# Storing only the combined weight operands of a seven-product FFN: quarters of the weights are loaded raw and split in either half of the sequence

## Chip, cores and metric

One core of a Trainium2 chip runs the whole kernel in one launch. The metric is the device time of a launch in microseconds; lower is better. Engines are named as in the profile: PE is TensorE, DVE VectorE, ACT ScalarE, POOL GpSimd, SP the queue engine that issues the DMAs (SyncE).

## What is computed

One layer of a streaming trunk on x of shape (1, 2048, 1024) in float32, D_FF = 2816:

```
h = rmsnorm(x); u = h @ w_in                       # 1024 -> 1536
y_lru  = rg_lru(conv(u[:512])) * gelu(u[512:1024])
y_pool = pool_mixer(u[1024:])
h_res = x + concat(rmsnorm(y_lru), rmsnorm(y_pool)) @ w_out
h = rmsnorm(h_res)
ff = silu(h @ ffn_w1) * (h @ ffn_w3)               # 1024 -> 2816, twice
out = rmsnorm(h_res + ff @ ffn_w2)                 # 2816 -> 1024
```

The change is in the FFN alone: the three products with `ffn_w1`, `ffn_w3` and `ffn_w2`.

## The kernel before, in words

**Precision.** A float32 product is made of three matmuls on a reduced type (fp32r). Each operand is split into a high part (a copy that rounds, on ScalarE) and a low part (source minus high part, on VectorE); `split` (L231) does that, and `mm3` (L236) multiplies high by high, high by low and low by high into one PSUM bank (L237, L238, L239 in this order).

**FFN.** The 2048 tokens are worked off in two halves (`hf` 0 and 1) of two chunks of 512 tokens. D_FF is cut into 11 column groups `j` of 256 columns (the loop at L893). For each group and half, `ffn_gate` (w1), `ffn_up` (w3) and `ffn2` (w2) each multiply a 2 x 2 block matrix of weights with a 2 x 2 block matrix of activations. They do so with seven block products (numbered n = 0 to 6) where the plain way takes eight, the scheme of Strassen in Winograd's form. The weight operands are the quarters b11, b21 and b22 themselves and four combinations of quarters, t1 to t4, which GpSimd makes by subtracting quarters (`comb`). In `ffn1` (L584, which serves gate and up) the products 0, 2 and 6 take b11, b21 and b22; in `ffn2` (L681) the products 2, 3 and 6 take b11, b21 and b22. VectorE and GpSimd combine the results: u2 and u3 (L630, L632, L636) in `ffn1`, and sums into `acc` and `G` (L706, L710) in `ffn2`; ScalarE brings products out of PSUM (`copy_a`, L224). The last group's w2 (`ffn2_last`, L767) takes four plain products, with four raw quarters.

**Where weights come from.** In half 0 the quarters are loaded raw (`load_raw`, L206, 256 KB each), combined, and split by `split_kept` (L198) into one of four 512 KB slots (pool "wsp", tile w_hl). The split operand is then stored to DRAM (c13_d for w1 and w3, c2_d for w2; c_d in the profile, L203). In half 1 nothing is combined or split: `kept` (L182) reads every operand back from there. Of each seven calls, three read it as two 256 KB halves into the slots for raw quarters (six slots, pool "raw"), the other four into one slot of "wsp" (the tiles w_kept).

**Order.** In the loop over groups the seven products of `ffn2(j)` and of `ffn_gate(j + 1)` alternate ("fg" seven times), after the seven of `ffn_up(j)`. At the change of halves the first products of the next half's gate stand ahead of `ffn2_last`. The order on each engine is made at build time by a list scheduler which simulates the program's time; `tc.high_priority(AHEAD)` raises the priority of splits and evictions by 400 (FIRST: by 1500). So an edit may move instructions on every engine. DMAs are issued by SP in order.

Of the kernel before, what the change touches and what calls it, by code (L numbers as in the profile page):

```python
# [13 lines left out]
ALU = mybir.AluOpType  # L14
# [3 lines left out]
P = 128  # L18
# [3 lines left out]
W = 512  # L22
NB = W // P
# [47 lines left out]
def trunk(ctx: ExitStack, tc: tile.TileContext, xT, w_io, w13, w2, gates, pool_w, w_inT, vecs,  # L71
# [126 lines left out]
    def split_kept(src, cache, prepare=AHEAD, eng=None):  # L198

        w_ = wsp("w_hl", (P, 2, W))  # L200
        with tc.high_priority(prepare):
            split(w_[:, 0], w_[:, 1], src, eng)
        nc.sync.dma_start(cache, w_.bitcast(F32))  # L203
        return w_[:, 0], w_[:, 1]

    def load_raw(src, shape):  # L206
# [377 lines left out]
    def ffn1(hf, j, w, ops, s, after):  # L584
# [3 lines left out]

        def quarter(r, c):
            return load_raw(w13[j, w, r, c], (P, NB, P)).rearrange("p k m -> p (k m)") if hf == 0 else None  # L590

# [7 lines left out]
        def product(n, ps, a, b, fresh):  # L599
            wh, wl = split_kept(b, c13_d[j, w, n]) if hf == 0 else kept(c13_d[j, w, n])  # L600
            for kk in range(NB):
# [4 lines left out]
        X, Y = bank("ps"), bank("ps")  # L606
        b11 = quarter(0, 0)
        product(0, X, A11, b11, True)
# [9 lines left out]
        yield  # L618
        b21 = quarter(1, 0)
        product(2, X, A12, b21, False)  # L620
# [17 lines left out]
        yield  # L638
        product(6, V, S4, b22, False)
        after((V, u2), 1)  # L640
# [40 lines left out]
    def ffn2(hf, j, s, acc, G):  # L681
# [3 lines left out]
        def quarter(r, c):  # L685
            return load_raw(w2[j, r, c], (P, W)) if hf == 0 else None

# [9 lines left out]
        def product(n, banks, a, b, fresh):  # L697
            wh, wl = split_kept(b, c2_d[j, n]) if hf == 0 else kept(c2_d[j, n])
            for dp, ps in enumerate(banks):
# [25 lines left out]
        Y = banks("pY")  # L725
        b22, b12 = quarter(1, 1), quarter(0, 1)
        product(0, Y, operand(half(ALU.subtract, a11, a21)), comb("t3", b22, b12, "r1"), True)
# [29 lines left out]
        yield  # L757
        product(6, V, operand(half(ALU.subtract, a12, s2, s2)), b22, False)
        add(V, c12, "V")
# [7 lines left out]
    def ffn2_last(hf, s, acc):  # L767
# [3 lines left out]
        for h in range(2):  # L771
            for b in range(2):
                cache = c2_d[NP - 1, 2 * h + b]
                ws.append(split_kept(load_raw(w2[NP - 1, b, h], (P, W)), cache, 0) if hf == 0
                          else kept(cache))
        f = {q: operand(s[q], tag) for q, tag in ((2, "f"), (3, "f"), (0, "up" if end else "e"),
# [185 lines left out]
```

## Time and profile before

| | |
|---|---|
| median of 3 runs | 1935.81 us (1935.36 to 1936.9) |
| profiled execution | 1939.97 us, its span 1938.2 us |
| mean granted TensorE clock | 0.977 of full speed |
| PE busy | 1832.8 us, 95% of the span |
| DVE busy | 1355.5 us, 70% |
| POOL busy | 928.5 us, 48% |
| ACT busy | 769.5 us, 40% |
| HBM | 275.36 MB read, 167.77 MB written |

The mixers come first. The FFN's first half runs to about 1200 us, and its second half ends about 50 us before the span does. All durations below come from the profiled execution, which has its own time; the median belongs to other executions of the same kernel. A busy share is an average over stages with different limits, so the rows further down are taken stage by stage: from one steady column group to the next, and around the change of halves.

### The profile page before, as it was taken

How to read it: one execution, taken by the hardware profiler on the slowest of the kernel's cores; microseconds unless marked ns; L12 is line 12 of the kernel's file. 1: busy time of each engine (PE TensorE's matmuls, PEld its weight loads, DVE VectorE, ACT ScalarE, POOL GpSimd, SP SyncE). 2: the span in 40 equal slices, each digit the busy share in tenths (PEclk: the TensorE clock that was granted, in tenths of full speed). 3: DMA queues.
4: the chain of work that ended last, by engine and by line, in shares of the span. 5: the costliest groups of instructions: out<-in, count | busy, mean ns of one | idle time of the engine just before them, and what ended most of it. 6: DMA issues, size and time to landing. Idle time of an engine off the chain costs nothing.

```text
span 1938.2 us, 23419 instructions
## 1 busy us (share of the span) xinstructions
PE 1832.8 (95%) x8016; PEld 1487.6 (77%) x8016; DVE 1355.5 (70%) x2004; ACT 769.5 (40%) x1294; POOL 928.5 (48%) x633
## 2 busy tenths in 40 slices
PE   7989999999988999999999999799999999999996
PEld 5778888787767777777777787577888888888885
DVE  7598499876669778777887878875444445444457
ACT  5463546362334444443444434442322223322223
POOL 3361723332136567666676668373333334432373
PEclk9999999999989999999999999899999999999998
DMA  9956855476987666566656666868555555555552
GB/s 322 321 206 219 323 201 179 148 288 227 394 328 260 227 246 223 217 238 220 245 210 231 230 246 230 313 206 298 186 197 194 195 187 183 201 190 195 195 174 87
DMA packets 160838, 444.69 MB, mean 229 GB/s; under 512 B 17872, under 2 KB 20048, under 8 KB 155728
## 3 DMA queue, kind: packets, MB, share of 16 engines
q1 hardware_dynamic: 160720, 443.20, 64.1%
q8 instruction: 63, 1.03, 0.2%
q14 instruction: 55, 0.45, 0.1%
HBM read 275.36 MB, written 167.77 MB: 229 GB/s over the span
## 4 chain that ended last, share of the span: by engine, by line
PE 69%; DVE 17%; issue 5%; DMA 3%; ACT 2%; POOL 2%; SPq 0%; DVEq 0%; ACTq 0%; POOLq 0%
PE ps L239 17%; PE ps L237 16%; PE ps L238 16%; DVE w_hl L234 3%; PE pV L238 2%; PE pV L239 2%; PE pV L237 2%; PE pX L237 2%; PE pX L238 2%; PE pX L239 2%; DMA c_d<-w_hl 1%; PE pY L237 1%; PE pY L238 1%; PE pY L239 1%; DVE sf L719 1%
## 5 line engine op out<-in xcount | busy, mean ns | idle before, releaser
L710 POOL TENSOR_TENSOR G<-G,e 128x512 f32<-128x512 f32 x152 | 227.8, 1516 | 132.1 <-ACT e L224 129.7
L239 PE MATMUL ps<-h_hi,w_hl 128*128 128x512 f32 x616 | 249.0, 405 | 26.2 <-DVE w_hl L234 26.0
L237 PE MATMUL ps<-h_hi,w_hl 128*128 128x512 f32 x616 | 245.5, 401 | 17.7 <-DVE u L636 10.2
L238 PE MATMUL ps<-h_lo,w_hl 128*128 128x512 f32 x616 | 244.9, 398 | 0.0
L237 PE MATMUL ps<-h_hi,w_kept 128*128 128x512 f32 x616 | 240.9, 392 | 2.0 <-DMA w_kept<-c_d 1.2
L238 PE MATMUL ps<-h_lo,w_kept 128*128 128x512 f32 x616 | 240.9, 391 | 0.0
L239 PE MATMUL ps<-h_hi,w_kept 128*128 128x512 f32 x616 | 238.8, 391 | 0.0
L291 POOL TENSOR_TENSOR sq<-sq 128x512 f32<-128x512 f32 (+1 forms) x71 | 99.7, 1407 | 167.0 <-ACT sq L288 165.6
L239 PEld LDWEIGHTS ps<-h_hi,w_hl 128*128 128x128 f32 x616 | 117.9, 191 | 65.7 <-DVE w_hl L234 40.9
L234 DVE TENSOR_TENSOR f_lo<-sf,f_hi 128x512 fp32r<-128x512 f32 x80 | 92.3, 1154 | 106.8 <-PE pZ L238 37.9
L237 PEld LDWEIGHTS ps<-h_hi,w_hl 128*128 128x128 f32 x616 | 118.0, 191 | 49.6 <-ACT w_hl L224 11.2
L710 POOL TENSOR_TENSOR acc<-acc,e 128x512 f32<-128x512 f32 x80 | 123.3, 1570 | 61.5 <-ACT e L224 60.2
L632 POOL TENSOR_TENSOR u<-u,u 128x512 f32<-128x512 f32 x44 | 66.1, 1502 | 179.2 <-DVE u L630 179.1
L706 DVE TENSOR_TENSOR acc<-pV,acc 128x512 f32<-128x512 f32 x160 | 107.9, 685 | 47.4 <-PE pV L239 46.6
L234 DVE TENSOR_TENSOR w_hl<-raw,w_hl 128x512 fp32r<-128x512 f32 x120 | 130.7, 1091 | 12.1 <-ACT w_hl L224 11.6
L238 PEld LDWEIGHTS ps<-h_lo,w_hl 128*128 128x128 f32 x616 | 118.1, 192 | 25.2
L237 PEld LDWEIGHTS ps<-h_hi,w_kept 128*128 128x128 f32 x616 | 115.8, 188 | 27.8 <-DVE acc L837 1.6
L239 PEld LDWEIGHTS ps<-h_hi,w_kept 128*128 128x128 f32 x616 | 115.7, 188 | 25.4 <-DMA w_kept<-c_d 0.3
L238 PEld LDWEIGHTS ps<-h_lo,w_kept 128*128 128x128 f32 x616 | 115.8, 188 | 25.0
L224 ACT ACTIVATE f_hi<-sf 128x512 fp32r<-128x512 f32 x80 | 50.6, 633 | 202.3 <-DVE sf L719 151.9
L224 ACT ACTIVATE w_hl<-t 128x512 fp32r<-128x512 f32 x96 | 60.3, 628 | 165.6 <-DMA c_d<-w_hl 83.2
L237 PE MATMUL ps<-x_hi,w_kept 128*128 128x512 f32 x288 | 115.0, 401 | 1.4 <-DVE u_g L388 1.4
(359 smaller groups left out, 4520.1 us busy)
## 6 DMA issues: line engine op xcount, KB each, us to landing
c_d<-w_hl SPq DMA_DIRECT2D x228, 512.0 KB, 2.9
w_kept<-c_d SPq DMA_DIRECT2D x130, 512.0 KB, 3.7
w_kept<-c_d SPq DMA_DIRECT2D x196, 256.0 KB, 3.4
w_kept<-cio_d SPq DMA_DIRECT2D x68, 512.0 KB, 3.9
raw<-w SPq DMA_DIRECT2D x132, 256.0 KB, 3.3
w_kept<-cio_d SPq DMA_DIRECT2D x104, 256.0 KB, 3.3
cio_d<-w_hl SPq DMA_DIRECT2D x40, 512.0 KB, 5.2
h_lo<-h_d SPq DMA_DIRECT2D x14, 1024.0 KB, 9.6
```

Source lines behind the costliest of these rows:

```text
L224: return nc.scalar.activation(out, in_, AF.Copy)
L234: (eng or nc.vector).tensor_tensor(lo, src, hi.bitcast(F32), ALU.subtract)
L237: i = nc.tensor.matmul(ps, wh, xh, start=first, stop=False, **kw)
L238: nc.tensor.matmul(ps, wh, xl, start=False, stop=False, **kw)
L239: nc.tensor.matmul(ps, wl, xh, start=False, stop=last, **kw)
L291: eng.tensor_tensor(total, total, sq, ALU.add)
L632: nc.gpsimd.tensor_tensor(u3, u3, u2, ALU.add)
L706: nc.vector.tensor_tensor(dst[dp], ps, dst[dp], ALU.add)
L710: nc.gpsimd.tensor_tensor(dst[dp], dst[dp], e, ALU.add)
L719: nc.vector.tensor_tensor(out, a, b, op)
```

## The change

A new function `operand_w` stands between the products and the two ways of getting a split operand. With a cache it does what was done before: split and store in half 0, read back in half 1. With `None` for a cache it splits the raw quarter into a "wsp" slot and stores nothing, in either half. `None` is given for the products 0, 2 and 6 of `ffn1`, for 2, 3 and 6 of `ffn2`, and for all four operands of `ffn2_last`. In half 1 those quarters are therefore loaded raw again (256 KB where 512 KB were read back) and split again.

```diff
--- before.py
+++ after.py
@@ -202,6 +202,15 @@
             split(w_[:, 0], w_[:, 1], src, eng)
         nc.sync.dma_start(cache, w_.bitcast(F32))
         return w_[:, 0], w_[:, 1]
+
+    def operand_w(hf, b, cache, prepare=AHEAD):
+
+        if cache is None:
+            w_ = wsp("w_hl", (P, 2, W))
+            with tc.high_priority(prepare):
+                split(w_[:, 0], w_[:, 1], b)
+            return w_[:, 0], w_[:, 1]
+        return kept(cache) if hf else split_kept(b, cache, prepare)
 
     def load_raw(src, shape):
         raw = pool.tile(list(shape), F32, name="raw", tag="raw", bufs=N_RAW)
@@ -586,8 +595,11 @@
 
         A11, S3, A12, A22 = ops[0]
 
-        def quarter(r, c):
-            return load_raw(w13[j, w, r, c], (P, NB, P)).rearrange("p k m -> p (k m)") if hf == 0 else None
+        def quarter(r, c, again=False):
+
+            if hf and not again:
+                return None
+            return load_raw(w13[j, w, r, c], (P, NB, P)).rearrange("p k m -> p (k m)")
 
         def comb(name, a, b, tag="up"):
             if hf:
@@ -597,14 +609,14 @@
             return t
 
         def product(n, ps, a, b, fresh):
-            wh, wl = split_kept(b, c13_d[j, w, n]) if hf == 0 else kept(c13_d[j, w, n])
+            wh, wl = operand_w(hf, b, None if n in (0, 2, 6) else c13_d[j, w, n])
             for kk in range(NB):
                 col = slice(kk * P, kk * P + P)
                 mm3(ps, wh[:, col], wl[:, col], a[0][:, kk], a[1][:, kk],
                     fresh and kk == 0, kk == NB - 1, skip_group_check=True)
 
         X, Y = bank("ps"), bank("ps")
-        b11 = quarter(0, 0)
+        b11 = quarter(0, 0, True)
         product(0, X, A11, b11, True)
         u2 = t2("u2", "tm")
         with tc.high_priority(AHEAD):
@@ -616,7 +628,7 @@
         with tc.high_priority(AHEAD):
             copy_a(u3, Y)
         yield
-        b21 = quarter(1, 0)
+        b21 = quarter(1, 0, True)
         product(2, X, A12, b21, False)
         after(X, 0)
         yield
@@ -636,7 +648,7 @@
             nc.vector.tensor_tensor(u3, V, u3, ALU.add)
         after((u3, None), 3)
         yield
-        product(6, V, S4, b22, False)
+        product(6, V, S4, quarter(1, 1, True) if hf else b22, False)
         after((V, u2), 1)
         yield
 
@@ -683,7 +695,7 @@
 
 
         def quarter(r, c):
-            return load_raw(w2[j, r, c], (P, W)) if hf == 0 else None
+            return load_raw(w2[j, r, c], (P, W))
 
         a11, a12, a21, a22 = (s[q] for q in range(4))
 
@@ -695,7 +707,7 @@
             return t
 
         def product(n, banks, a, b, fresh):
-            wh, wl = split_kept(b, c2_d[j, n]) if hf == 0 else kept(c2_d[j, n])
+            wh, wl = operand_w(hf, b, None if n in (2, 3, 6) else c2_d[j, n])
             for dp, ps in enumerate(banks):
                 col = slice(P * dp, P * (dp + 1))
                 mm3(ps, wh[:, col], wl[:, col], a[0], a[1], fresh, True, skip_group_check=True)
@@ -723,7 +735,10 @@
         c11, c12, c21, c22 = acc[0][0:NB], acc[0][NB:], acc[1][0:NB], acc[1][NB:]
 
         Y = banks("pY")
-        b22, b12 = quarter(1, 1), quarter(0, 1)
+        if hf == 0:
+            b22, b12 = quarter(1, 1), quarter(0, 1)
+        else:
+            b22 = b12 = None
         product(0, Y, operand(half(ALU.subtract, a11, a21)), comb("t3", b22, b12, "r1"), True)
         add(Y, c22, "P")
         yield
@@ -755,7 +770,7 @@
         product(5, V, operand(s1), t1, True)
         add(V, c22, "V")
         yield
-        product(6, V, operand(half(ALU.subtract, a12, s2, s2)), b22, False)
+        product(6, V, operand(half(ALU.subtract, a12, s2, s2)), quarter(1, 1) if hf else b22, False)
         add(V, c12, "V")
         yield
 
@@ -770,9 +785,7 @@
         ws = []
         for h in range(2):
             for b in range(2):
-                cache = c2_d[NP - 1, 2 * h + b]
-                ws.append(split_kept(load_raw(w2[NP - 1, b, h], (P, W)), cache, 0) if hf == 0
-                          else kept(cache))
+                ws.append(operand_w(hf, load_raw(w2[NP - 1, b, h], (P, W)), None, 0))
         f = {q: operand(s[q], tag) for q, tag in ((2, "f"), (3, "f"), (0, "up" if end else "e"),
                                                   (1, "up" if end else "f"))}
         scales = []
```

The scheduler's order changes with it. In the rows below a name's number tells tiles apart, and line numbers of the changed kernel are 9 to 12 higher (L234 is L243, L224 is L233, L596 is L608, L632 is L644).

**GpSimd in the first half**, a steady column group, where it makes the combinations of the gate's quarters (t1, t2_) and, with u3, the running sum of `ffn_up`. Before:

```order
L596 TENSOR_TENSOR t1_7084<-raw_6982,raw_6926 128x512
L632 TENSOR_TENSOR u3_6778<-u3_6778,u2_6754 128x512
L596 TENSOR_TENSOR t2__7086<-raw_6980,t1_7084 128x512
L694 TENSOR_TENSOR t4_6958<-raw_6952,t2__6950 128x512
L671 TENSOR_TENSOR s_6688<-s_6688,u3_6778 128x512
```

With the change:

```order
L608 TENSOR_TENSOR t1_7047<-raw_6948,raw_6893 128x512
L608 TENSOR_TENSOR t2__7049<-raw_6946,t1_7047 128x512
L644 TENSOR_TENSOR u3_6747<-u3_6747,u2_6723 128x512
L706 TENSOR_TENSOR t4_6924<-raw_6918,t2__6916 128x512
L683 TENSOR_TENSOR s_6660<-s_6660,u3_6747 128x512
```

The combination t2_ has moved ahead of u3.

**VectorE in the same group**, from the last addition to u3 to the split of the gate's t3 (sf and f are activations on their way into `ffn2`, w_hl the weight operands). Before:

```order
L636 TENSOR_TENSOR u3_6778<-ps_6822,u3_6778 128x512
L719 TENSOR_TENSOR sf_6888<-s_6532,s_6639 128x512
L234 TENSOR_TENSOR f_lo_6891<-sf_6888,f_hi_6890 128x512
L234 TENSOR_TENSOR w_hl_6960<-t4_6958,w_hl_6960 128x512
L719 TENSOR_TENSOR sf_7106<-s_6639,s_6688 128x512
L234 TENSOR_TENSOR f_lo_6955<-s_6688,f_hi_6954 128x512
L719 TENSOR_TENSOR sf_7108<-sf_7106,s_6532 128x512
L670 TENSOR_TENSOR u2_6754<-ps_6822,u2_6754 128x512
L234 TENSOR_TENSOR w_hl_6986<-t3_6984,w_hl_6986 128x512
```

With the change:

```order
L648 TENSOR_TENSOR u3_6747<-ps_6790,u3_6747 128x512
L731 TENSOR_TENSOR sf_6855<-s_6505,s_6611 128x512
L243 TENSOR_TENSOR w_hl_6926<-t4_6924,w_hl_6926 128x512
L243 TENSOR_TENSOR f_lo_6858<-sf_6855,f_hi_6857 128x512
L731 TENSOR_TENSOR sf_7069<-s_6611,s_6660 128x512
L243 TENSOR_TENSOR f_lo_6921<-s_6660,f_hi_6920 128x512
L731 TENSOR_TENSOR sf_7071<-sf_7069,s_6505 128x512
L243 TENSOR_TENSOR w_hl_6952<-t3_6950,w_hl_6952 128x512
L682 TENSOR_TENSOR u2_6723<-ps_6790,u2_6723 128x512
```

The low part of t4 now stands ahead of f_lo, and that of t3 ahead of u2's last addition.

**ScalarE in the second half**, between two evictions of `ffn_up` (u3 and u2). Before:

```order
L224 ACTIVATE u3_12995<-ps_12962 128x512
L224 ACTIVATE f_hi_13089<-sf_13087 128x512
L224 ACTIVATE f_hi_13139<-s_12917 128x512
L224 ACTIVATE u2_13137<-ps_13119 128x512
L224 ACTIVATE f_hi_13183<-s_12773 128x512
L224 ACTIVATE e_13107<-pY_13083 128x512
```

With the change:

```order
L233 ACTIVATE w_hl_13529<-raw_13527 128x512
L233 ACTIVATE u3_13454<-ps_13418 128x512
L233 ACTIVATE w_hl_13586<-raw_13584 128x512
L233 ACTIVATE f_hi_13552<-sf_13550 128x512
L233 ACTIVATE f_hi_13607<-s_13369 128x512
L233 ACTIVATE u2_13601<-ps_13582 128x512
L233 ACTIVATE w_hl_13655<-raw_13603 128x512
L233 ACTIVATE f_hi_13651<-s_13226 128x512
L233 ACTIVATE w_hl_13684<-raw_13682 128x512
L233 ACTIVATE e_13570<-pY_13546 128x512
```

Four copies into weight operands now stand among the evictions and the activations' splits. At the change of halves TensorE's order moves too: twelve matmuls of the next half's gate (its product 0, on h_hi and h_lo of the new tokens) now stand between the products 2 and 6 of the old half's last `ffn_up`, where those two were neighbours.

## Rows read from the trace of the kernel before

**Rows 1.** By stretch: us, PE, PEld, DVE, ACT, POOL, clock, DMA share, GB/s.

```profile
621.00:1180.00 559.00, 533.47 (x2272) 424.14 (x2271) 453.63 (x531) 243.41 (x432) 381.59 (x239) 0.99 0.63 229
1383.50:1843.60 460.10, 460.10 (x2018) 378.43 (x2017) 220.87 (x304) 128.10 (x217) 165.47 (x121) 1.00 0.56 192
```

**Rows 2.** Timeline of ScalarE (start, us, [idle before]): once per column group.

```profile
745.48 0.58 ACT L652 ACTIVATE s<-ps 128x512 f32<-128x512 f32 x1
...
807.39 0.58 ACT L652 ACTIVATE s<-ps 128x512 f32<-128x512 f32 x1
...
1442.37 0.60 ACT L652 ACTIVATE s<-ps 128x512 f32<-128x512 f32 x1 [2.66 <-PE ps L239]
...
1557.39 0.60 ACT L652 ACTIVATE s<-ps 128x512 f32<-128x512 f32 x1 [2.66 <-PE ps L239]
```

**Rows 3.** Waits (total, times, longest): 600-1200 us; third row 1310-1880.

```profile
PE ps L239 <- DVE w_hl L234: 22.2, 21, 2.5
PE ps L237 <- ACT w_hl L224: 5.7, 7, 1.1
...
PE pY L237 <- ACT f_hi L224: 1.9, 1, 1.9
...
ACT w_hl L224 <- DMA c_d<-w_hl: 83.0, 27, 5.1
```

**Rows 4.** Timeline of TensorE: the three stalls of one group.

```profile
788.37 0.50 PE L239 MATMUL ps<-h_hi,w_hl 128*128 128x512 f32 x1 [0.74 <-DVE w_hl L234]
...
798.18 0.50 PE L239 MATMUL ps<-h_hi,w_hl 128*128 128x512 f32 x1 [0.95 <-DVE w_hl L234]
...
803.87 0.50 PE L239 MATMUL ps<-h_hi,w_hl 128*128 128x512 f32 x1 [1.32 <-DVE w_hl L234]
```

**Rows 5.** Timeline of VectorE in the same group.

```profile
784.48 0.69 DVE L630 TENSOR_TENSOR u<-ps,u 128x512 f32<-128x512 f32 x1 [4.16 <-PE ps L239]
...
792.42 1.00 DVE L234 TENSOR_TENSOR f_lo<-sf,f_hi 128x512 fp32r<-128x512 f32 x1 [0.70 <-ACT f_hi L224]
793.34 0.68 DVE L234 TENSOR_TENSOR w_hl<-t,w_hl 128x512 fp32r<-128x512 f32 x1
...
802.06 1.76 DVE L234 TENSOR_TENSOR w_hl<-raw,w_hl 128x512 fp32r<-128x512 f32 x1
```

**Rows 6.** Timeline of SP, TensorE and ScalarE around one store.

```profile
803.84 0.32 SPq L203 DMA_DIRECT2D c_d<-w_hl  x1
...
806.07 0.40 PE L239 MATMUL ps<-h_hi,w_hl 128*128 128x512 f32 x1
...
806.85 0.63 ACT L224 ACTIVATE w_hl<-t 128x512 fp32r<-128x512 f32 x1 [2.95 <-DMA c_d<-w_hl]
```

**Rows 7.** Timeline of SP and GpSimd: a raw load and the combinations behind it.

```profile
780.72 0.45 SPq L208 DMA_DIRECT2D raw<-w  x1
...
784.77 1.29 POOL L596 TENSOR_TENSOR t<-raw 128x512 f32<-128x512 f32 x1 [8.37 <-DMA raw<-w]
786.03 1.74 POOL L632 TENSOR_TENSOR u<-u,u 128x512 f32<-128x512 f32 x1
```

**Rows 8.** Busy time, opening; TensorE's longest wait, 1205 to 1310 us.

```profile
581.50:629.90 48.40, 42.87 (x177) 34.19 (x178) 45.52 (x50) 20.69 (x38) 29.19 (x19) 0.96 0.71 260
...
PE ps L237 <- DVE u L636: 7.9, 1, 7.9
```

**Rows 9.** Groups (busy, mean ns | idle): 625-1180 us; two from 1383.5-1843.6.

```profile
L234 DVE TENSOR_TENSOR w_hl<-raw,w_hl 128x512 fp32r<-128x512 f32 x81 | 95.3, 1176 | 2.8 <-ACT w_hl L224 2.8
...
L234 DVE TENSOR_TENSOR f_lo<-sf,f_hi 128x512 fp32r<-128x512 f32 x32 | 30.9, 967 | 81.4 <-PE pZ L238 29.2 <-issue 20.4 <-ACT e L224 20.3
...
L706 DVE TENSOR_TENSOR acc<-pV,acc 128x512 f32<-128x512 f32 x64 | 44.2, 692 | 37.9 <-PE pV L239 37.8
```

**Rows 10.** DMA issues from 1383.5 to 1843.6 us (KB each, median us to landing).

```profile
w_kept<-c_d SPq DMA_DIRECT2D x97, 512.0 KB, 3.4
```

**Rows 11.** Timeline of VectorE near the end.

```profile
1887.47 0.69 DVE L636 TENSOR_TENSOR u<-ps,u 128x512 f32<-128x512 f32 x1
```

## The prediction, made before the changed kernel was run

> **What bounds the kernel now.** I read the busy time by stretch first. In the second half of the FFN, TensorE is busy for all of the 460.1 us of eight steady column groups, at full clock: 2018 matmuls in 460.1 us are 0.228 us each [rows 1]. In the first half it is busy 533 of 559 us, VectorE 454 and GpSimd 382; in the second VectorE has 221 of 460 and ScalarE 128 [rows 1]. The timeline of one instruction that comes once per column group gives the periods: 807.39 - 745.48 = 61.9 us in the first half, (1557.39 - 1442.37) / 2 = 57.5 us in the second [rows 2]. The matmuls are the same 252, so the first half loses 61.9 - 57.5 = 4.4 us a group, the second nothing. The waits say to whom: from 600 to 1200 us TensorE idles 22.2 + 5.7 us for the split of a weight operand, from 1310 to 1880 us only 1.9 us in all [rows 3].
>
> One period shows how. TensorE stops three times, at 788.37, 798.18 and 803.87 us, each time for the low part of a split (VectorE) [rows 4]. VectorE had no slack there: from u2 at 784.48 to the end of the split at 802.06 + 1.76 = 803.82 us it works through some 18 instructions with one gap of 0.70 us [rows 5], and TensorE goes on at 803.87. So a period of the first half is this VectorE chain, 19.4 us, and then 42.5 us in which TensorE doesn't wait. The second half is TensorE's alone: any wait there is paid in full.
>
> **Removed.** 100 stores of 512 KB go: 66 of w1 and w3 (11 groups, two matrices, three operands), 30 of w2, 4 of the last group. The built order has 128 such stores where there were 228. ScalarE waits 83.0 us for stores to land before it may write a split's slot [rows 3], which looks like the prize. It isn't: at 806.85 ScalarE starts after waiting 2.95 us for a store, but that store, issued at 803.84, covers a slot that TensorE itself reads until 806.07 + 0.40 = 806.47 [rows 6]. Without the store the slot is free 0.3 us earlier. I take nothing for it; for the other end see the second rival.
>
> **Moved, first half.** The raw load at 780.72 [rows 7] is issued right behind a store that the change removes; GpSimd waits 8.37 us for it and starts at 784.77 [rows 7]. It may now land up to about a microsecond sooner. In the built order GpSimd does the combination t2 ahead of u3: u3 then ends at 784.77 + 1.3 + 1.7 + 1.7 = 789.5 us even if the load is no earlier, before VectorE wants it (from the row at 786.03, and its duration, [rows 7]). On VectorE the split of t4 moves ahead of f_lo, into the 0.70 us gap, and so no longer stands behind it at 793.34 [rows 5]: 0.6 us off the chain, less 0.1 us because f_lo may start that much later. All the other splits and their number stay. That is -0.5 us for 10 periods, **-5 us**. Bounds: -10 (the stall at 798.18 goes too) and +3 (GpSimd's earlier start lengthens VectorE's instructions: the same split takes 1.76 us beside it and 0.68 without [rows 5]).
>
> **Opening and the change of halves.** Between 581.5 and 629.9 us the DMA queues are 0.71 busy and TensorE 42.9 us of 48.4 [rows 8]; some three in seven of the stores fall away, but VectorE is busy there for 45.5 us, so I take **-2 us** (0 to -6). At the change of halves TensorE waits 7.9 us once, for VectorE's u (L636) [rows 8]. The built order puts the gate's first product, 12 matmuls or 12 x 0.228 = 2.7 us, ahead of that wait, and one split more (0.7 us) ahead of u on VectorE: -2 us. The last seven of ten stores (3.5 MB) also leave the queues just when the next half's activations are read, against three further splits. Together **-2 us** (-6 to +4).
>
> **Added, second half.** 100 read-backs of 512 KB become 100 raw loads of 256 KB, each with a ScalarE copy (0.63 us [rows 6]) and a VectorE subtract. A subtract of this shape takes 1.18 us in the first half, where GpSimd is busy; the nearest of the second half, f_lo, takes 0.97 [rows 9]. Per eight groups, 72 of each: ScalarE 128 + 45 = 173 us, VectorE 221 + 70 = 291 of 460. Both have room, so the work itself costs nothing; its lateness can. In the built order 18 of these splits get their slot 20 matmuls (4.6 us) or less before it is read. In the first half of before about seven in each period have as short a time, some 68 from 600 to 1200 us, and cost (22.2 + 5.7) / 68 = 0.41 us each [rows 3]. At that price 18 cost 7 us. But those costs come from the back-to-back chain on VectorE, which the second half has not; copy and subtract fit into even 12 matmuls (2.7 us) when the engines are free: 0.63 + 0.97 = 1.6 us. The read-backs that stay come closer too: the shortest has 15 matmuls (3.4 us) from slot to use, where 25 was the least for that size, and lands in 3.4 us [rows 10]; three of these may cost 0.3 us each. I take **+3 us**, near the low end; bounds 0 and +16 (18 at 0.9 us, the stall at 788.37 with its slow restart).
>
> The Trainium skill (SBUF — State Buffer, Who interferes with whom) speaks against this term: a VectorE instruction with two SBUF inputs contends with a GpSimd instruction that reads SBUF, and whichever starts second waits for all of the other. Every added subtract is of that kind. The trace agrees in direction: 1.18 us for such a subtract against 0.69 us for an add that reads PSUM [rows 9]. By that rule alone the added subtracts would take the 1.18 us, VectorE 306 of 460 us, and the sum would stay as it is.
>
> **End.** Four operands of the last group are split where they were read back. u at 1887.47 is the last VectorE instruction before TensorE's final stretch [rows 11]; one or two subtracts of 0.69 us stand just ahead of that chain: **+1.5 us** (0 to +3).
>
> **Sum.** -5 - 2 - 2 + 3 + 1.5 = -4.5 us. The profiled execution took 1939.97 us, so 1935.5 by it; it stands 4.2 us over the median of the runs, 1935.81. The forecast is **1931.3 us**. About 0.2% (3.9 us) is what a measurement here can tell from no change; the forecast lies just beyond it.
>
> **Rivals.**
> - Slower: the second half starves. TensorE there has no gap to give. If the 18 late splits cost 0.5 us or more each, as the stalls at 788.37 and 798.18 do, that is +9 to +16, the first half's gain is eaten, and with the end the time is 1940 to 1948, say 1944. For it: zero slack and in-order ScalarE, where the new copies stand between evictions and copies that wait for VectorE. Against: half the load on VectorE. 0.25.
> - Much faster: the slots were the limit after all, and the first half falls half of its way to 57.5 us: 10 x 2.2 = 22 us more, 1909. For it: 83 us of waits for stores. Against: rows 6, and the splits that set the chain remain. The Trainium skill (Perfetto Trace Analysis, Optimization Strategy) says that the same gap coming back on the engine that should be saturated can mean too little SBUF for the next tile; the three stalls of each period would be such a gap, and stores that hold the four slots a cause. The trace speaks against it with the 0.3 us of rows 6. 0.08.
> - No difference: the VectorE chain keeps its length because GpSimd's work slides along with it, and the other terms cancel: 1935.5. 0.30.
> - That the change doesn't do what it says: the built order has 128 stores, 183 read-backs (326 before) and 232 raw loads (132). No chance given.
>
> **Numbers.** The forecast's case, 4 to 12 us faster, has 0.37, with the second rival 0.45 for faster; same 0.30; slower 0.25. The bounds added up would be -22 and +26; not all come together. The range 1918 to 1946 leaves out the second rival and the worst of the first.
>
> **What would show it.** Right: periods of about 61.4 us in the first half with the stall at the third split still there; 57.5 to 58 us in the second, VectorE near 290 of 460 us; about 50 MB less written. Wrong: second-half periods above 58.5 us with TensorE waiting for w_hl there (first rival), or first-half periods below 60 (second).

## The result and the profile after

The changed kernel takes 1947.88 us (median of 4 runs, 1946.89 to 1951.69) against 1936.36 us before (1935.36 to 1937.06): a ratio of 1.0064, 95% interval 1.0046 to 1.0081. It is 11.5 us slower, where 4.5 us less were forecast. The profiled execution took 1946.89 us, its span is 1945.1 us.

The change did what it says. From the page of the changed kernel, engine totals (busy time, share, instructions) and HBM traffic:

```profile
PE 1832.9 (94%) x8016; PEld 1486.7 (76%) x8016; DVE 1461.4 (75%) x2104; ACT 820.5 (42%) x1394; POOL 938.3 (48%) x633
...
HBM read 249.15 MB, written 115.34 MB: 187 GB/s over the span
```

100 stores are gone (167.77 MB written before), the 100 splits are there (DVE x2104), and TensorE's work is what it was. So the 11.5 us are waiting, or matmuls at a lower clock. To find them I take one instruction that comes once per column group and half, the SiLU of the gate's first quarter, and cut the span at its 2nd, 11th and 22nd start. The timeline of ScalarE shows them (start, duration; compare [rows 2]):

```profile
620.80 0.58 ACT L664 ACTIVATE s<-ps 128x512 f32<-128x512 f32 x1
...
1185.41 0.58 ACT L664 ACTIVATE s<-ps 128x512 f32<-128x512 f32 x1
...
1850.06 0.60 ACT L664 ACTIVATE s<-ps 128x512 f32<-128x512 f32 x1 [0.68 <-PE ps L248]
```

The four stretches between the start, these three cuts and the end, for every profiled kernel of this study (us; the ratio is that of all timed runs to those of the kernel before, on the same chip; the profile is of one run):

| profile | to the 2nd | nine periods of half 0 | turn and half 1 | end | span | ratio, 95% interval |
|---|---|---|---|---|---|---|
| before | 624.1 | 556.6 | 662.8 | 94.6 | 1938.2 | |
| before, again | 620.6 | 555.8 | 661.2 | 94.6 | 1932.1 | 0.9999 (0.9985 to 1.0014) |
| changed | 620.8 | 564.6 | 664.7 | 95.0 | 1945.1 | 1.0064 (1.0046 to 1.0081) |
| changed, again | 618.7 | 568.7 | 664.7 | 94.3 | 1946.5 | 1.0063 (1.0048 to 1.0078) |
| half0_nostore | 626.4 | 568.8 | 662.5 | 94.5 | 1952.2 | 1.0067 (1.0044 to 1.0090) |
| half1_raw | 621.8 | 555.6 | 666.7 | 94.0 | 1938.1 | 1.0026 (1.0013 to 1.0038) |
| pool_order | 622.8 | 551.4 | 665.6 | 94.3 | 1934.1 | 0.9989 (0.9976 to 1.0002) |
| u3_first_t3_first | 620.9 | 566.1 | 666.0 | 94.4 | 1947.4 | 1.0061 (1.0041 to 1.0082) |
| t3_behind_u2 | 621.4 | 554.2 | 671.3 | 94.2 | 1941.1 | 1.0028 (1.0016 to 1.0040) |
| before_t2first | 625.8 | 565.0 | 662.8 | 94.6 | 1948.1 | 1.0064 (1.0049 to 1.0079) |
| b21_pool | 622.0 | 546.4 | 668.8 | 94.0 | 1931.2 | 0.9983 (0.9969 to 0.9997) |
| b21_pool_before | 624.2 | 555.2 | 664.3 | 94.6 | 1938.3 | 1.0011 (1.0000 to 1.0022) |
| w2_raw | 621.6 | 555.4 | 667.0 | 95.8 | 1939.8 | 1.0028 (1.0012 to 1.0043) |
| last_only | 622.6 | 556.0 | 662.4 | 98.1 | 1939.0 | 1.0019 (1.0009 to 1.0029) |
| nolast_order | 621.0 | 551.2 | 665.2 | 94.3 | 1931.7 | 0.9978 (0.9968 to 0.9988) |
| w13_order | 619.3 | 550.8 | 666.6 | 91.6 | 1928.3 | 0.9966 (0.9956 to 0.9975) |
| w13_b21_order | 617.3 | 548.3 | 669.3 | 91.6 | 1926.5 | 0.9970 (0.9959 to 0.9982) |

By the means of the two profiles each, the changed kernel's first stretch is 2.6 us shorter, its nine periods are 10.5 us longer, the turn and second half 2.7 us longer, and the end is the same.

The cuts are starts on ScalarE, and they don't fall on the same matmul of TensorE in every version. The busy time of the nine periods shows it (us; then the engines in the order of [rows 1], instructions in brackets; the second profile of before, the first of the changed kernel):

```profile
620.56:1176.32 555.76, 529.89 (x2261) 420.99 (x2260) 450.17 (x529) 242.32 (x431) 382.13 (x239) 1.00 0.63 229
620.80:1185.41 564.61, 533.29 (x2275) 427.04 (x2274) 474.90 (x534) 242.65 (x435) 375.88 (x239) 0.99 0.43 152
```

The changed kernel's nine periods hold 14 matmuls more, and at 0.228 us each [rows 1] that is 3.2 us of the 10.5. The difference sits in the first of the nine: 62.9 and 64.1 us against 59.3 and 59.2. The other eight hold 252 matmuls each (251 once) and take 501.7 and 504.6 us against 497.3 and 496.5, 6.2 us more by the means. Corrected in this way by the matmuls that each stretch holds, the first stretch is 1.0 us shorter, the nine periods are 7.3 us longer, the turn and second half 3.6 us (seven matmuls fewer at the turn, three more behind it) and the end 0.8 us (three fewer). So about two thirds of the loss lie in the first half, where no work was added.

What happens there is in the timeline of TensorE, one group of the changed kernel (start, duration, [idle before, releaser]). It answers to [rows 4]:

```profile
787.14 0.50 PE L248 MATMUL ps<-h_hi,w_hl 128*128 128x512 f32 x1 [0.81 <-DVE w_hl L243]
...
795.85 0.50 PE L248 MATMUL ps<-h_hi,w_hl 128*128 128x512 f32 x1
...
802.83 0.50 PE L248 MATMUL ps<-h_hi,w_hl 128*128 128x512 f32 x1 [2.60 <-DVE w_hl L243]
803.16 0.40 PE L246 MATMUL ps<-h_hi,w_hl 128*128 128x512 f32 x1
...
804.46 0.63 PE L248 MATMUL ps<-h_hi,w_hl 128*128 128x512 f32 x1
804.89 0.63 PE L246 MATMUL pY<-f_hi,w_hl 128*128 128x512 f32 x1
```

The stall for the gate's t3 (795.85), 0.95 us before, is nearly gone. The last one, for b21, has grown from 1.32 to 2.60 us. The waits for a split, 22.2 and 5.7 us in [rows 3], are 32.9 us now (TensorE, 600 to 1200 us), and around the change of halves a read-back is late (1310 to 1885 us):

```profile
PE ps L248 <- DVE w_hl L243: 32.9, 24, 2.6
...
PE ps L246 <- DMA w_kept<-c_d: 4.8, 3, 4.3
```

Behind the stall the matmuls above start 0.43 us apart (804.46, 804.89) instead of 0.23. That is the clock. The busy time by stretch of the changed kernel's second profile shows the same place in two groups, 4 us from the end of the stall on (granted clock in the third column from the end):

```profile
803.87:807.87 4.00, 4.00 (x18) 3.31 (x19) 3.64 (x6) 0.50 (x1) 1.09 (x1) 1.00 0.46 133
866.43:870.43 4.00, 4.00 (x11) 3.18 (x12) 2.19 (x3) 0.00 (x0) 1.04 (x1) 0.59 0.46 131
```

In one group the clock stays at its upper level (2.4 GHz) and 18 matmuls start; in the other it is at the lower level (1.2 GHz) for most of the stretch and 11 start. Before both, TensorE had idled the same 2.6 us. The time that the matmuls between 0.40 and 0.46 us apart lose against 0.23 is 1.0 to 1.6 us in such a group. There are three such groups among nine in the first profile of the changed kernel and five in the second, with periods of 63.4 to 64.3 us beside 61.9 to 62.9 us for the rest. The kernel before has one or two such groups, but there the clock falls at the second of its stalls, the third vanishes in return, and the period stays at 62.0 to 62.2 us. At the last stall of a group nothing is left to be taken up by it. Where the clock stays up, one of the eight equal groups takes 62.2 us in the changed kernel and 62.1 before, by the means: measured against before, nearly all of the loss in these groups is the fall of the clock.

### The profile page after: what moved, and what is told of

It is laid out like the page before. It is cut to its first block, busy times and chain, and to the rows that moved or that the text cites. A ratio compares the mean times of both kernels' runs of the same rounds, so it can differ in the third digit from the quotient of the medians.

```text
span 1945.1 us, 23362 instructions
## 1 busy us (share of the span) xinstructions
PE 1832.9 (94%) x8016; PEld 1486.7 (76%) x8016; DVE 1461.4 (75%) x2104; ACT 820.5 (42%) x1394; POOL 938.3 (48%) x633
## 4 chain that ended last, share of the span: by engine, by line
PE 67%; DVE 19%; issue 5%; DMA 4%; POOL 4%; ACT 2%; SPq 0%; DVEq 0%; POOLq 0%; ACTq 0%
PE ps L248 16%; PE ps L246 16%; PE ps L247 16%; DVE w_hl L243 3%; PE pV L247 2%; PE pV L248 2%; PE pV L246 2%; PE pX L247 2%; PE pX L248 2%; PE pX L246 2%; DVE s L683 2%; DVE sf L731 2%; DVE f_lo L243 2%; PE pY L246 1%; PE pY L247 1%
## 5 line engine op out<-in xcount | busy, mean ns | idle before, releaser
L248 PE MATMUL ps<-h_hi,w_hl 128*128 128x512 f32 x880 | 352.8, 402 | 40.0 <-DVE w_hl L243 39.4
L246 PE MATMUL ps<-h_hi,w_hl 128*128 128x512 f32 x880 | 347.8, 397 | 6.1 <-ACT h_hi L233 2.5
L247 PE MATMUL ps<-h_lo,w_hl 128*128 128x512 f32 x880 | 348.1, 396 | 2.8 <-DVE h_lo L243 2.8
L243 DVE TENSOR_TENSOR w_hl<-raw,w_hl 128x512 fp32r<-128x512 f32 x220 | 219.6, 999 | 27.2 <-ACT w_hl L233 25.2
L248 PEld LDWEIGHTS ps<-h_hi,w_hl 128*128 128x128 f32 x880 | 167.4, 190 | 92.3 <-DVE w_hl L243 57.1
L233 ACT ACTIVATE w_hl<-raw 128x512 fp32r<-128x512 f32 x240 | 149.3, 625 | 202.1 <-PE ps L248 175.5
L246 PEld LDWEIGHTS ps<-h_hi,w_hl 128*128 128x128 f32 x880 | 168.0, 191 | 45.2 <-ACT h_hi L233 3.3
L644 POOL TENSOR_TENSOR u<-u,u 128x512 f32<-128x512 f32 x44 | 69.5, 1580 | 223.1 <-DVE u L642 221.6
L246 PE MATMUL ps<-h_hi,w_kept 128*128 128x512 f32 x352 | 137.1, 394 | 4.9 <-DMA w_kept<-c_d 4.8
L233 ACT ACTIVATE w_hl<-t 128x512 fp32r<-128x512 f32 x96 | 60.4, 630 | 189.1 <-PE ps L248 78.9
L248 PE MATMUL ps<-h_hi,w_kept 128*128 128x512 f32 x352 | 138.4, 393 | 0.0
L247 PE MATMUL ps<-h_lo,w_kept 128*128 128x512 f32 x352 | 138.2, 393 | 0.0
L608 POOL TENSOR_TENSOR t<-raw 128x512 f32<-128x512 f32 x44 | 72.1, 1650 | 122.0 <-DMA raw<-w 66.0
L243 DVE TENSOR_TENSOR f_lo<-sf,f_hi 128x512 fp32r<-128x512 f32 x80 | 92.8, 1161 | 38.5 <-PE pX L247 20.6
L246 PE MATMUL ps<-x_hi,w_kept 128*128 128x512 f32 x288 | 114.6, 400 | 1.3 <-DVE u_g L397 1.3
L248 PE MATMUL ps<-x_hi,w_kept 128*128 128x512 f32 x288 | 114.8, 400 | 0.0
L247 PE MATMUL ps<-x_lo,w_kept 128*128 128x512 f32 x288 | 113.6, 397 | 0.0
```

Of the source, the lines that this page charges most:

```text
L233: return nc.scalar.activation(out, in_, AF.Copy)
L243: (eng or nc.vector).tensor_tensor(lo, src, hi.bitcast(F32), ALU.subtract)
L246: i = nc.tensor.matmul(ps, wh, xh, start=first, stop=False, **kw)
L247: nc.tensor.matmul(ps, wh, xl, start=False, stop=False, **kw)
L248: nc.tensor.matmul(ps, wl, xh, start=False, stop=last, **kw)
L608: nc.gpsimd.tensor_tensor(t, a, b, ALU.subtract)
```

## The experiments

**The theories.** A: the order that the scheduler chose for the first half makes the loss. B: the late splits of the second half make it (the first rival). Later A was divided further.

### The two kernels once more

> The kernel before, once more, for a second profile. Theory A (the new order of the first half costs) and theory B (the late splits of the second half cost) both expect 1935 to 1938 us. The profiled execution of before stood 4 us over its median; if that was chance, this profile has a span near 1935 and the missing 3 us lie in the first half or at the change of halves, since the second half had no excess to lose.

> The changed kernel once more: 1946.5 to 1949 us by both theories. Theory A: 3 to 4 us of the difference to before lie between 620 and 1180 us, where VectorE is again busy 17 us longer. Theory B: the larger part lies behind 1300 us.

Measured: 1935.35 us (ratio 0.9999) and 1947.16 us (1.0063). The second profile of before is 6.1 us shorter than the first: 3.5 us ahead of the second cut, 0.8 us in the nine periods, 1.6 us behind. So the prediction's profiled execution had chance losses mostly in the opening, and differences of 3 us there tell nothing between single profiles. The nine periods of the two profiles agree to 1 us for before and to 4 us for the changed kernel, whose clock falls in three groups of one and in five of the other. Theory A had put 3 to 4 us into the first half: right in place, too small in size. VectorE, too, is busy longer in the first half: 474.90 us of 564.6 (changed) against 450.17 of 555.8 (before, again).

### One half of the change at a time

half0_nostore, on the kernel before (`split_only` is `split_kept` without its store; w2 and the last group alike):

```diff
-wh, wl = split_kept(b, c13_d[j, w, n]) if hf == 0 else kept(c13_d[j, w, n])
+raw = {0: 1, 2: 3, 6: 5}
+if hf:
+    wh, wl = kept(c13_d[j, w, raw.get(n, n)])
+else:
+    wh, wl = split_only(b) if n in raw else split_kept(b, c13_d[j, w, n])
```

half1_raw, on the changed kernel (w2 and the last group alike):

```diff
-wh, wl = operand_w(hf, b, None if n in (0, 2, 6) else c13_d[j, w, n])
+wh, wl = operand_w(hf, b, None if hf and n in (0, 2, 6) else c13_d[j, w, n])
```

> Half 0 of the changed kernel (no stores of the quarters), half 1 of before: the 100 operands that were not stored are replaced in half 1 by reading back a neighbouring product's operand of the same size, so that no raw load and no split is added; the FFN's result of half 1 is another one. Theory A: 1940 to 1944 us (+4 to +8, the loss is in the first half and at the change of halves). Theory B: 1932 to 1936 us, no slower than before.

> Half 0 of before (all operands stored, 100 of the stores for nothing), half 1 of the changed kernel (100 raw loads and splits). Theory A: 1939 to 1942 us (+3 to +6: two or three late read-backs and splits, and the end). Theory B: 1945 to 1949 us, nearly all of the difference.

Measured: 1946.66 us (ratio 1.0067) and 1941.19 us (1.0026). The built order of half 0 is that of the changed kernel in the first and that of before in the second, on every engine. So half 0 alone costs as much as the whole change, more than theory A's 1940 to 1944 us: 568.8 us for nine periods, though stores only went away there and the order followed (the profile is of the slowest of its four runs, 1953.99 us). Half 1 costs some 5 us, within theory A's range and all behind the nine periods (666.7 against 662 us). Theory B falls as the main cause. The two halves, +13 and +5 us, add up to more than the whole change, +12 us on that chip; the intervals are too wide (half0_nostore's spans 9 us) to say whether that means anything.

### Which move of the order

In the changed kernel's order two things moved near the long stall and are tested here: GpSimd makes t2 ahead of u3, and VectorE subtracts the low part of t3 ahead of ffn_up's last u2 (both are in the order shown with the change). A constraint between two instructions of one engine undoes either. pool_order holds GpSimd's t2 behind u3; the scheduler then puts t3 behind u2 by itself:

```diff
-nc.gpsimd.tensor_tensor(t, a, b, ALU.subtract)
+i = nc.gpsimd.tensor_tensor(t, a, b, ALU.subtract)
+if w == 0 and name == "t2_" and "u3" in last:
+    issue_after(i, last["u3"])
...
-nc.gpsimd.tensor_tensor(u3, u3, u2, ALU.add)
+i = nc.gpsimd.tensor_tensor(u3, u3, u2, ALU.add)
+if w:
+    last["u3"] = i
```

> The changed kernel with one constraint more: in ffn_gate GpSimd makes t2 only behind the u3 of ffn_up, as in the order of before; all operations and DMAs are those of the changed kernel. In the built order VectorE's u2 then stands ahead of the split of t3 again. Theory A, now narrower (the new order puts the stalls of a group into one of 2.76 us, behind which the clock falls in about half of the groups): the stalls are 1.1 and 1.5 us again, the period of the first half is 62.0 us, the time 1938 to 1942 us. Theory C (the missing stores themselves do it, by what lands earlier): as the changed kernel, 1945 to 1949 us.

Measured: 1934.97 us, ratio 0.9989, with the same operations and DMAs as the changed kernel. The nine periods take 551.4 us, 13 to 17 us less than the changed kernel's and 5 us less than before's (the eight equal ones 491.2 us, 12 and 5.7 us less by the means). The order makes the loss, as theory A says, and C falls. But the time is 3 us below theory A's range: the first of the three stalls of [rows 4] is gone, too, which A had not foreseen (more on it below). To see which of the two moves it is, u3_first_t3_first adds one constraint to that version (`issue_after(last["up"], last["lo"])`: the u2 behind the subtract of t3):

> The changed kernel with GpSimd's u3 ahead of t2 (as before) and VectorE's split of t3 ahead of the last u2 (as in the changed kernel). Theory V (VectorE's order alone makes the long stall): stalls of 2.6 us in every group, some with a fall of the clock behind them; nine periods take 560 to 569 us where the version with GpSimd's order alone took 551, and the time is 1942 to 1949 us. Rival H (it takes both moves together): 551 to 556 us, 1933 to 1938 us.

Measured: 1949.30 us, ratio 1.0061, nine periods 566.1 us (the eight equal ones 504.5). VectorE's move makes the loss without GpSimd's. The constraint is one place, but the scheduler moved more with it: on VectorE a split of a raw quarter now stands ahead of the product s<-s,u, as in the changed kernel, and behind the long stall one combination on GpSimd and a few matmuls change places. The timelines show how it costs. pool_order, TensorE's two stalls of a group:

```profile
796.31 0.50 PE L248 MATMUL ps<-h_hi,w_hl 128*128 128x512 f32 x1 [0.95 <-DVE w_hl L243]
...
802.00 0.50 PE L248 MATMUL ps<-h_hi,w_hl 128*128 128x512 f32 x1 [1.31 <-DVE w_hl L243]
```

and its VectorE (u2, split of t3, product with u2, a raw split, and the split that ends the last stall) and GpSimd (t4, then additions to acc):

```profile
794.98 0.68 DVE L686 TENSOR_TENSOR u<-ps,u 128x512 f32<-128x512 f32 x1
795.58 0.68 DVE L243 TENSOR_TENSOR w_hl<-t,w_hl 128x512 fp32r<-128x512 f32 x1
796.18 0.68 DVE L687 TENSOR_TENSOR s<-s,u 128x512 f32<-128x512 f32 x1
796.78 1.78 DVE L243 TENSOR_TENSOR w_hl<-raw,w_hl 128x512 fp32r<-128x512 f32 x1
...
800.19 1.76 DVE L243 TENSOR_TENSOR w_hl<-raw,w_hl 128x512 fp32r<-128x512 f32 x1
...
796.33 1.68 POOL L608 TENSOR_TENSOR t<-raw,t__7049 128x512 f32<-128x512 f32 x1 [2.43 <-DVE w_hl L243]
797.97 6.83 POOL L726 TENSOR_TENSOR acc<-acc,e 128x512 f32<-128x512 f32 x4
```

The same of u3_first_t3_first, TensorE first, then VectorE and GpSimd:

```profile
795.46 0.50 PE L248 MATMUL ps<-h_hi,w_hl 128*128 128x512 f32 x1 [0.36 <-DVE w_hl L243]
...
802.46 0.50 PE L248 MATMUL ps<-h_hi,w_hl 128*128 128x512 f32 x1 [2.62 <-DVE w_hl L243]
```

```profile
794.73 0.68 DVE L243 TENSOR_TENSOR w_hl<-t,w_hl 128x512 fp32r<-128x512 f32 x1
795.33 0.68 DVE L688 TENSOR_TENSOR u<-ps,u 128x512 f32<-128x512 f32 x1
795.93 1.40 DVE L243 TENSOR_TENSOR w_hl<-raw,w_hl 128x512 fp32r<-128x512 f32 x1
797.25 1.78 DVE L691 TENSOR_TENSOR s<-s,u 128x512 f32<-128x512 f32 x1
...
800.65 1.75 DVE L243 TENSOR_TENSOR w_hl<-raw,w_hl 128x512 fp32r<-128x512 f32 x1
...
795.49 1.29 POOL L608 TENSOR_TENSOR t<-raw,t__7049 128x512 f32<-128x512 f32 x1 [1.83 <-DVE w_hl L243]
796.73 6.82 POOL L730 TENSOR_TENSOR acc<-acc,e 128x512 f32<-128x512 f32 x4
```

GpSimd's t4 waits for the split of t3. With t3 behind u2, the product s<-s,u starts 0.15 us ahead of t4 and takes 0.68 us, and the raw split behind it 1.78. With t3 ahead, t4 starts while VectorE is still at u2; the raw split (1.40 us) and the product (1.78 us) both come among them: 3.18 us where they took 2.46. The two stalls, 0.95 + 1.31 us, become 0.36 + 2.62 us: the same 0.7 us more in all, 6 us for nine periods. Most of the rest of the 14.7 us between the two versions is the clock behind the longer stall, 1.4 to 1.7 us in four of the nine groups, against 0.4 us at most in any group of pool_order. That the raw split has changed places with the product costs nothing by itself: in the next run it stands ahead of the product, too, but t3 behind u2, and the two take 0.68 + 1.78 us again (795.86 and 796.46 us in its trace).

> The changed kernel with one constraint: the low part of the gate's t3 is subtracted behind ffn_up's last u2 on VectorE, as in the order of before; GpSimd keeps t2 ahead of u3. Theory G: 1944 to 1949 us, as the changed kernel. Theory V: stalls of 1.1 and 1.5 us, periods of 61 to 62.1 us, 1933 to 1939 us.

> The kernel before with all its stores, and one constraint: GpSimd's u3 of ffn_up comes behind the gate's t2, as in the built order of the changed kernel. VectorE's split of t3 stays behind the last u2. Theory G (GpSimd's order makes the long stall, since it collides with VectorE otherwise): stalls of 2.7 us, 1942 to 1947 us. Theory V (VectorE's order makes it, t3 ahead of u2): stalls of 1.1 and 1.5 us, 1934 to 1939 us.

t3_behind_u2 is the changed kernel with the one constraint `issue_after(last["lo"], last["up"])`. Measured: 1941.30 us, ratio 1.0028, above its range; but the nine periods take 554.2 us (the eight equal ones 493.2) with no stall over 1.5 us in them, as theory V has it. What holds the total up is another stretch, the turn and second half with 671.3 us. before_t2first (the constraint of pool_order the other way round, on the kernel before) took 1950.13 us, ratio 1.0064: above the range of either theory, and not in the way of theory G. Its waits of TensorE over the nine periods, and in one group GpSimd's part of u3 and VectorE's u3 (L640) with the addition ahead of it:

```profile
PE ps L239 <- DVE w_hl L234: 19.7, 27, 1.3
PE ps L237 <- DVE u L640: 12.7, 9, 1.4
```

```profile
792.97 1.74 POOL L634 TENSOR_TENSOR u<-u,u 128x512 f32<-128x512 f32 x1
...
795.29 1.66 DVE L723 TENSOR_TENSOR sf<-s 128x512 f32<-128x512 f32 x1
796.87 0.68 DVE L640 TENSOR_TENSOR u<-ps,u 128x512 f32<-128x512 f32 x1
```

Here TensorE waits nine times for u3. GpSimd's part of it, behind t1 and t2, ends at 794.71 us, when VectorE is still at work on the instruction before; but VectorE then does sf<-s (1.66 us) and only after it u3. In the order of before, and in that of the changed kernel, u3 stands ahead of sf<-s, and no such wait shows. So the scheduler answered this constraint with another move on VectorE, and the run doesn't show what GpSimd's order alone costs where the stores are: the 8.8 us (565.0 against 556.2) are of both moves, and 2.7 us of them are 12 matmuls more in the nine periods. Where the stores are gone, GpSimd's order, with what was moved along, costs 2.8 us (554.2 against 551.4) and VectorE's 14.7 us.

### One subtract of each group on GpSimd

b21_pool on the changed kernel (`split` is given `eng=nc.gpsimd` for half 0, gate, n = 2), b21_pool_before the same on the kernel before.

> The changed kernel, but in half 0 the low part of the gate's third operand (b21, the split that ends the longest stall) is subtracted on GpSimd and not on VectorE. Theory A says that VectorE's chain sets the first half: 1.75 us less on it per group, and up to the whole stall of 2.76 us: 10 x 1.7 to 10 x 3.5 us with the clock, so 1913 to 1930 us. Rival D (VectorE and GpSimd hold each other up, so that a subtract costs the same on either): 1943 to 1950 us, with a stall at the same place.

> The kernel before with that one subtract per group on GpSimd. Theory A: the stall of 1.48 us goes and some of the 1.12 us: 10 to 25 us less, 1911 to 1926 us. Rival D: 1933 to 1940 us.

Measured: 1933.32 us (ratio 0.9983) and 1939.28 us (1.0011). The first lies between the two ranges, the second in that of rival D. On the changed kernel the nine periods shrink to 546.4 us, the shortest of all, and the clock falls vanish; 4 us go again at the turn. On the kernel before the last stall falls from 1.32 to 0.63 us, but a new one of 0.4 us appears at another place in eight of the nine groups and the period stays (555.2 us). So one subtract less on VectorE is worth 18 to 22 us of the nine periods in one order and next to nothing in the other: VectorE's total isn't the bound by itself. That it is decided by which instructions meet on the two engines would fit both, but no run shows it apart.

### Which weights, and a version that beats both

w2_raw: only the quarters of w2 and the last group's four are raw. last_only: only those four. nolast_order: pool_order with those four stored and read back. w13_order: pool_order with all of w2 stored and read back:

```diff
-wh, wl = operand_w(hf, b, None if n in (2, 3, 6) else c2_d[j, n])
+wh, wl = operand_w(hf, b, c2_d[j, n])
...
-ws.append(operand_w(hf, load_raw(w2[NP - 1, b, h], (P, W)), None, 0))
+ws.append(operand_w(hf, None if hf else load_raw(w2[NP - 1, b, h], (P, W)), c2_d[NP - 1, 2 * h + b], 0))
```

w13_b21_order adds the subtract on GpSimd to w13_order.

> Only the quarters of w2 and the last group's four operands are loaded raw and split twice; all operands of w1 and w3 are stored and read back. The built order of the first half is that of before on every engine. Theory A: first half as before, at most the late read-backs and the end remain: 1934 to 1940 us. Theory C: 34 of the 100 stores fall away, and so a third of the loss: 1938 to 1941 us with periods over 62.3 us.

> Only the last group's four w2 operands are loaded raw and split in both halves; everything else is as before. Theory E (what the raw splits cost behind 1200 us is the change of halves, where the four splits of ffn2_last and the next half's first operands get into each other's way): 1938 to 1942 us, the loss between 1180 and 1360 us, nothing behind it. Theory F (it is the quarters of ffn2 in the second half): 1935 to 1937.5 us.

> The changed kernel with GpSimd's u3 ahead of t2 again, and with the last group's four operands stored and read back as before. Theory E: 2 to 5 us under the version with the order alone, 1930 to 1934 us. Theory F: the same as it, 1934 to 1936 us.

> Only the quarters of w1 and w3 are loaded raw and split twice, with GpSimd's u3 ahead of t2; all of w2 is stored and read back as before. By the order theory the first half keeps its 61.0 us per group (the built order there is the same). Theories E and F both: 1929 to 1934 us, 3 to 7 us faster than before; E expects it to equal the run without the last group's part, F expects it 2 to 5 us below that one.

> As the run with only w1 and w3 raw and the order restored, and in half 0 the low part of the gate's b21 is subtracted on GpSimd. If GpSimd's subtract takes work off the chain in this order as in the changed kernel's (60.7 us per group there, 61.0 by the order alone), the two gains add and the period is 60 to 60.7 us: 1923 to 1931 us. If they are two ways to the same place: 1929 to 1935 us.

w2_raw: 1942.23 us, ratio 1.0028, above its range; the first half is that of before (555.4 us), the loss behind it. last_only: 1940.78 us, ratio 1.0019, and not where theory E had put it: the end takes 98.1 instead of 94.6 us. TensorE waits there for a u that stands behind the splits on VectorE (1841 us to the end):

```profile
PE ps L246 <- DVE u L648: 2.9, 1, 2.9
```

In the changed kernel as a whole that wait is 1.0 us, so this price depends on the order too. w2_raw and last_only keep before's order in the first half with 34 and 4 stores fewer, and their nine periods are before's (555.4 and 556.0 us): these missing stores alone change nothing there. nolast_order: 1932.50 us, ratio 0.9978; its interval meets that of pool_order, so what the four cost there stays open. w13_order: 1930.05 us, **ratio 0.9966 (0.9956 to 0.9975), faster than both kernels**. It stands 2.4 us below nolast_order on the same chip, but the two intervals meet, so theories E and F aren't told apart. Its first half has pool_order's order and 550.8 us. Its end looks 3 us shorter because the last cut falls 13 matmuls later (366 behind it instead of 379). The subtract on GpSimd adds nothing to it (0.9970): nine periods fall by 2.5 us and the turn gives them back.

## Why the prediction was wrong

- **What bounds the kernel** was right: TensorE waits for splits in the first half and for next to nothing in the second.
- **Removed stores, nothing for ScalarE's 83 us of waits**: right in its place. With 34 stores fewer and the same order (w2_raw) the nine periods are those of before, and the second rival's 22 us never came, in any version. The Trainium skill (Perfetto Trace Analysis, Optimization Strategy) says that a gap that comes back can mean too few buffers; here the gaps moved and changed size with the order alone, with four slots throughout.
- **Moved, first half, -5 us: the step that failed.** It was worked out from the t4 and t2 moves and held that "all the other splits and their number stay". The order on record also shows t3 ahead of u2, and I gave that no term. VectorE's product and raw split behind it, before and in the changed kernel:

```profile
798.05 0.68 DVE L671 TENSOR_TENSOR s<-s,u 128x512 f32<-128x512 f32 x1
798.65 1.79 DVE L234 TENSOR_TENSOR w_hl<-raw,w_hl 128x512 fp32r<-128x512 f32 x1
```

```profile
796.32 1.39 DVE L243 TENSOR_TENSOR w_hl<-raw,w_hl 128x512 fp32r<-128x512 f32 x1
797.63 1.77 DVE L683 TENSOR_TENSOR s<-s,u 128x512 f32<-128x512 f32 x1
```

  The two take 3.16 us instead of 2.47. The forecast's gain of 0.5 us is eaten (VectorE's chain from u2 to the end of the last split takes 19.5 to 19.6 us by the mean of eight groups, 19.2 to 19.3 before), the waiting comes together in one stall of 2.6 us, and the clock falls behind it in eight of 18 groups: +10.5 us over nine periods, +7.3 us for the same matmuls, where -4.5 were forecast. The upper bound of +3 held the first effect at a fraction and had no place for the clock.

  The moves that did get a term were sized well. t3_behind_u2 keeps both and takes back that of t3: its chain is 18.8 us, 0.5 us shorter than before as forecast, and its eight equal groups take 3.7 us less than before's. pool_order takes back those two moves as well (a steady group has before's order on VectorE), and its chain is shorter still, 18.5 us. There the raw load lands sooner: GpSimd's t1 starts 0.9 us ahead of u2 instead of 0.3 us behind it, and the next split on VectorE takes 0.68 us, in before's group of [rows 5] 1.53 us (pool_order, then before):

```profile
782.53 1.30 POOL L608 TENSOR_TENSOR t<-raw 128x512 f32<-128x512 f32 x1 [6.79 <-DMA raw<-w]
783.46 0.69 DVE L644 TENSOR_TENSOR u<-ps,u 128x512 f32<-128x512 f32 x1 [4.16 <-PE ps L248]
784.07 0.68 DVE L243 TENSOR_TENSOR w_hl<-t,w_hl 128x512 fp32r<-128x512 f32 x1
```

```profile
785.09 1.53 DVE L234 TENSOR_TENSOR w_hl<-t,w_hl 128x512 fp32r<-128x512 f32 x1
```

- **Opening, -2 us**: -2.6 us between means, -1.0 us for the same matmuls, within the scatter of two profiles. Not settled.
- **Change of halves -2, second half +3 us**: together +2.7 us measured, +3.6 us for the same matmuls. From the 14th start of the SiLU to the 22nd, eight groups, before takes 460.1 us and the changed kernel 462.4 and 462.7 us with three matmuls more: +1.7 us, so the second half's term was near. The turn takes the same time with seven matmuls fewer: +1.8 us where -2 were forecast. In the steady second half the forecast of load was good: VectorE 284.96 and ScalarE 165.75 of 460.9 us (forecast 291 and 173), and a split takes 0.85 us:

```profile
1387.60:1848.50 460.90, 460.47 (x2013) 377.25 (x2013) 284.96 (x377) 165.75 (x288) 170.92 (x120) 1.00 0.45 150
```

```profile
L243 DVE TENSOR_TENSOR w_hl<-raw,w_hl 128x512 fp32r<-128x512 f32 x72 | 60.9, 846 | 8.2 <-ACT w_hl L233 7.6 <-DMA w_kept<-c_d 0.6
```

  No matmul waits there for a late split, so the first rival, whose 1940 to 1948 us hold the measured time, had the wrong mechanism: its number is luck. The gain at the turn was wrong: the old wait for u (7.9 us) went, and a read-back that lands late (4.3 us) and waits for the next half's splits came.
- **End, +1.5 us**: 0 in the changed kernel (+0.8 us for the same matmuls), 3.5 us in last_only.
- **The sum** was set against a profiled execution 4.2 us above its median. The second profile shows that 3.5 of them were chance in the opening, so that correction was sound.

What stays open: the turn and second half take 661 to 671 us by version. Nearly all of that spread lies between the 11th and the 14th start (201 to 209 us); the eight groups behind take 460 to 464 us in every version. Waits of 3 to 5 us change at the turn with each built order, and no run separated them. Why the clock falls behind one stall of 2.6 us and not behind the next wasn't found either.

## What to carry to other kernels

Where a scheduler orders the engines, an edit's cost is that of the new order, and the operations that were added or removed can be the smaller part: compare the order around each stall row by row, and give a term to every row that changed places, not to those that help. One constraint between two instructions can then be worth more than the edit; it can also move others, so compare again before you read its time. Several short stalls were cheaper here than one long one of nearly the same sum (62.1 us a group against 62.2 with the clock up and 63.4 to 64.3 where it fell), above all because the long one is the last of its period, where the fall is paid in full. And cuts for a comparison by stage must hold the same work: count the matmuls between them first.

## What the runs showed of the hardware that was not expected

- After one and the same idle time of 2.6 us the granted clock fell in some groups (0.59 over the next 4 us) and not in others (1.00), three and five times in nine in two profiles of one program. Most of the 4 us between that program's nine periods in the two executions (564.6 and 568.7 us) is this. In pool_order and t3_behind_u2, with last stalls of 1.3 us, it fell in none of 18 groups.
- A VectorE product of two SBUF tiles takes 0.68 us when it starts 0.15 us ahead of a GpSimd instruction, and 1.78 us when GpSimd is already at work. The Trainium skill (SBUF — State Buffer, Who interferes with whom) says that the order of issue decides which of the two waits. The trace agrees: in the first case GpSimd's t4 takes 1.68 us, in the second, where it started first, 1.29 us. A change of places on VectorE alone turned it.
